# Holding the reads of turned blocks, row sums and meta probabilities until two to three gaps after an attention head

## The chip, the cores and the metric

The kernel runs on one core of one Trainium2 chip. Its engines work side by side, each through its own list of instructions in order: TensorE (PE, matmuls), VectorE (DVE), ScalarE (ACT), GpSimd (POOL) and SyncE (SP). SP only issues DMA transfers. An engine that waits for a semaphore holds everything behind it on its own list. The metric is the device time of one execution in microseconds; several runs are given by their median.

## The reference

Two layers of a decoder trunk over 512 tokens and 16 learned meta tokens put ahead of them, width 1024, float32. Per layer:

```
h = rmsnorm(x)
[u_pool | z_pool | c_q | c_kv | k_rope | z_mla | g_pool | g_mla] = h @ W_in
y_pool = W_pool_up( pool_mix(u_pool) * silu(z_pool) )
y_mla  = W_mla_up( mla(c_q, c_kv, k_rope) * silu(z_mla) )
x = x + W_out( sigmoid(g_pool) * y_pool + sigmoid(g_mla) * y_mla )
```

`mla` is causal attention with 8 heads: queries and keys of 64 + 32 features (32 of them rotary), values of 64, the query and key rows normalised, a softmax over all earlier tokens and the meta tokens. The result drops the meta positions.

## The kernel before

All activations lie transposed, features on the 128 partitions and the 528 tokens along the free axis. To keep float32 accuracy at a fast matmul rate, each operand is split into a rounded high part and the rest, and each product is three matmuls (`mm3`, lines 202 to 204): high by high, high by low, low by high. `wload` (line 189) does that for a 128x512 tile of weights: a DMA brings `raw` (line 133, three buffers), ScalarE makes `whi` (line 197), VectorE makes `wlo` (line 198).

The large products of both layers stand in one list, and `stream` walks it as a generator, a few matmuls at a step. The attention heads are written around it: wherever a head would have to wait, it calls `gap`, which advances the generator by a set amount of planned time (`FILL`, 2620 and 2530 ns in layers 0 and 1). `clk` adds up this planned time; `after(ns, fn)` puts a function on a list that `step` runs once `clk` has passed its time. So the program text is emitted as a mixture of heads and products. A scheduler then sets the order on each engine from its own estimate of when things are ready; the order is fixed in the program before it runs. `behind(a, b)` makes instruction `a` wait for instruction `b`; `newest[0]` is the last matmul that `mm3` emitted.

One head (`head`, line 805) goes like this. TensorE makes the scores of the four blocks of 128 queries against all their keys, VectorE masks them and finds the row maxima (`top`, line 824), ScalarE takes the exponential and sums the rows into `rs` (`expo`, line 831). `turn` (line 833) copies the 16 meta columns into `pm` on POOL (line 834) and transposes the rest on VectorE in squares of 32x32 into `attD` (line 837; one buffer). The squares reach their right partitions through DRAM: four stores `pdr<-attD` (line 899) and one read `attE<-pdr` of 640 KB (line 901; two buffers). The row sums go to DRAM as a row, `rdr<-rs` (line 894, 2 KB), and come back spread over 64 partitions, `cq<-rdr` (line 902, the tile `rb`). After an odd head `meta_turn` (line 909) sends the meta probabilities of the pair the same way: `mdr<-cq` (line 916) and three reads `racc<-mdr` (line 918). Then POOL multiplies the gate `z` by the reciprocal row sums (line 906), which waits for `cq<-rdr`.

Between heads, `prep` (line 783) moves parts of keys and queries with small transfers (`kh`, `kl`, `qhl`, lines 797 to 801). One head later `parts` (line 921) splits what was read into `attE`, and `pv` (line 932) multiplies it with the values; after an odd head, some time later, a matmul with `racc` (line 965) adds the meta part, and the result is multiplied by `z` (line 969).

All of these transfers, and the weight loads, stand on SP's one list. Each transfer signals one of eight semaphores in turn, so a transfer also waits for the one eight before it.

At the very start `WARM` matmuls of ones (line 155) run while the first data are on their way.

Of the kernel before, what the change touches and what calls it, by code (L numbers as in the profile page):

```python
# [9 lines left out]
F32 = mybir.dt.float32  # L10
F32R = mybir.dt.float32r
# [7 lines left out]
P = 128  # L19
# [3 lines left out]
NM = 16  # L23
T = SEQ + NM
# [30 lines left out]
LAG = 2000.0  # L55
TAIL = (9000.0, 9000.0)
SPL = 240
RET = 12500.0
WARM = 8
NB = 10  # L60


# [16 lines left out]
def trunk(ctx, tc, xT, xrow, mrow, pos, win, wkr, wqb, wkb, wvb, wgr, wpu, wmu, wout, gains, const, yT):  # L79
    nc = tc.nc  # L80
    pe, act, dve, gp, sp = nc.tensor, nc.scalar, nc.vector, nc.gpsimd, nc.sync
# [11 lines left out]
    def nm(s):  # L93
        uid[0] += 1
        return f"{s}_{uid[0]}"

    def slot(tag, dt=F32, bufs=1, w=W):
        return sl.tile([P, w], dt, tag=tag, name=nm(tag), bufs=bufs)
# [4 lines left out]
    def att(tag):  # L103
        return sl.tile([P, NB * P], F32 if tag == "D" else F32R, tag=f"att{tag}", name=nm(f"att{tag}"), bufs=1 if tag == "D" else 2)

    def wide():
        return tp.tile([P, NB * P], F32R, tag="th", name=nm("th"), bufs=2)
# [45 lines left out]
    wps = pp.tile([P, 512], F32, tag="o", name="wps", bufs=1)  # L153
    for i in range(WARM):
        pe.matmul(wps[:, 0:P], ones, ones, start=True, stop=True)
# [51 lines left out]
    newest = [None]  # L207
# [60 lines left out]
    def after(ns, fn):  # L268
        pend.append((clk[0] + ns, fn))
        pend.sort(key=lambda e: e[0])  # L270
# [32 lines left out]
    def behind(ins, other):  # L303
        tc.add_manual_dep(ins.ins, other.ins.name,
                          mybir.DependencyInfo(mybir.DependencyClass.Sync, mybir.DependencyReason.DATA))
# [35 lines left out]
    class Layer:  # L341
# [58 lines left out]
        def norm_sums(self):  # L400
# [51 lines left out]
            self.inv, self.cinv = slot("rinv"), slot("q1")  # L452
            fill_now(RET / 2)
            if self.l == 0:
                tables()
            fill_now(RET / 2 if self.l else RET / 4)
            for i, d in enumerate((self.inv, self.cinv)):
# [347 lines left out]
        def head(self, h, kq, prev):  # L805
            kh, kl, qh, ql = kq
            odd = h % 2
            nqs = self.nqs
            pa, pb, pc = slot("pa", w=416), slot("cq8"), slot("cq10")
            bia = sm.tile([P, 5], F32, tag="bia", name=nm("bia"), bufs=2)  # L810
            rs = sm.tile([P, 5], F32, tag="rs", name=nm("rs"), bufs=2)
            if odd == 0:
                self.pm = sm.tile([P, 4, 32], F32, tag="pm", name=nm("pm"), bufs=2)
                self.rb = slot("cq11")
            pm, rb = self.pm, self.rb
            blocks = att("D")
            grid = blocks.rearrange("p (b s r) -> p b s r", b=4, s=NB)

            def scores(i, out, a, b):
                q0 = NM + P * i  # L820
                return mm3(out, qh[:, q0:q0 + P], ql[:, q0:q0 + P], kh[:, a:b], kl[:, a:b], True, True)

            def top(i, c, sv, mask):
                return dve.tensor_tensor_reduce(out=sv, in0=sv, in1=mask, scale=nqs[:, i, h:h + 1], scalar=3e38,  # L824
                                                op0=ALU.add, op1=ALU.min, accum_out=bia[:, c:c + 1])

            def causal(n):
                return maskw[:, 512 - n:]

            def expo(i, c, sv, pv):  # L830
                act.activation(pv, sv, AF.Exp, scale=-1.0, bias=bia[:, i:i + 1], accum_out=rs[:, c:c + 1])  # L831

            def turn(i):
                gp.tensor_copy(pm[:, i, 16 * odd:16 * odd + 16], pt[i][:, 0:NM])  # L834
                for j, n in ((0, i + 1),) if i in (0, 1, 3) else ((0, 2), (2, 1)):
                    k = block(i, j)
                    ins = dve.transpose(grid[:, :, k:k + n, :].rearrange("p b s r -> p s b r"), pt[i][:, NM + P * j:NM + P * (j + n)])  # L837
                    if i in (1, 2):
                        behind(ins, newest[0])

            pt = [pa[:, 0:144], pa[:, 144:416], pb[:, 0:400], pc[:, 0:T]]
            sa = sct()
            s1, s3 = sa[:, 0:272], sa[:, 272:272 + SPL]
            scores(1, s1, 0, 272)
            scores(3, s3, 0, SPL)
            top(1, 1, s1, causal(272))
            top(3, 4, s3, maskw[:, 0:SPL])
            sb = sct()
            s2 = sb[:, 0:400]
            scores(2, s2, 0, 400)  # L850
            top(2, 2, s2, causal(400))
            expo(1, 1, s1, pt[1])
            expo(2, 2, s2, pt[2])
            if h == 1:
                self.spread_rope(1)
            if odd == 0 and h + 2 < H:
                self.spread_k(h // 2 + 1)
            self.gap()
            turn(1)
            turn(2)  # L860
            self.pv(prev)
            if h == 2:
                self.rope_keys(1)
            if odd and h + 1 < H:
                behind(self.keys(h // 2 + 1), newest[0])
            self.gap()
            sc = sct()
            s0, s4 = sc[:, 0:144], sc[:, 144:144 + T - SPL]
            scores(3, s4, SPL, T)

            def passes(out, q0, n):
                return [lambda k=k, q=q, x=x: pe.matmul(out, q[:, q0], x[:, 0:n], start=k == 0, stop=k == 2)
                        for k, (q, x) in enumerate(((qh, kh), (qh, kl), (ql, kh)))]

            todo = passes(s0, slice(NM, NM + P), 144)
            if not self.last:
                sm_ = sc[0:NM, 432:432 + NM]
                todo += passes(sm_, slice(0, NM), NM)
            for fn in todo:
                fn()  # L880
            if not self.last:
                dve.tensor_add(self.smeta[:, h, :], sm_, cst[0:NM, C_MM:C_MM + NM])
            top(3, 3, s4, causal(T - SPL))
            top(0, 0, s0, causal(144))
            dve.tensor_tensor(out=bia[:, 3:4], in0=bia[:, 3:4], in1=bia[:, 4:5], op=ALU.min)
            expo(3, 4, s3, pt[3][:, 0:SPL])
            expo(3, 3, s4, pt[3][:, SPL:T])
            expo(0, 0, s0, pt[0])
            turn(3)
            turn(0)  # L890
            dve.tensor_add(rs[:, 3:4], rs[:, 3:4], rs[:, 4:5])
            dve.reciprocal(rs[:, 0:4], rs[:, 0:4])
            row = rdr[self.l][h]
            sp.dma_start(row.rearrange("a (p i) -> p (a i)", i=4), rs[:, 0:4])
            got = att("E")
            n = NB * 32
            via = pdr[h % 2]
            for a in range(4):
                sp.dma_start(via[:, n * a:n * a + n].rearrange("(b k) x -> k b x", k=32),
                             blocks[32 * a:32 * a + 32, :].rearrange("p (b x) -> p b x", x=n))  # L900
            sp.dma_start(got.bitcast(F32), via)
            sp.dma_start(rb[64 * odd:64 * odd + 64, 0:512], row.partition_broadcast(64))
            if odd == 1:
                self.meta_turn(pm)
                z = self.zms[h // 2][:, NM:T].rearrange("p (i q) -> p i q", i=4)
                gp.tensor_mul(z, z, rb[:, 0:512].rearrange("p (q i) -> p i q", i=4))  # L906
            return h, got

        def meta_turn(self, pm):
            t = slot("cq9", F32R)  # L910
            f, hi, lo = t[:, 0:P], t[:, P:2 * P], t[:, 2 * P:3 * P]
            dve.transpose(f.bitcast(F32), pm.rearrange("p i r -> p (i r)"))
            split(hi, lo, f.bitcast(F32), 0, P)
            self.mt = slot("racc", F32R)
            via = mdr[0]
            sp.dma_start(via, t[:, P:3 * P].bitcast(F32))
            for g, c in ((0, 0), (32, 1), (64, 0)):
                sp.dma_start(self.mt[g:g + 32, 0:512].bitcast(F32).rearrange("p (a x) -> p a x", a=4),
                             via[:, P * c:P * c + P].rearrange("(a r) x -> r a x", a=4))

        def parts(self, prev):
            if prev is None:
                return None
            h, got = prev
            hi, f = wide(), got.bitcast(F32)
            for a in (0, NB * 64):
                b = a + NB * 64
                behind(act.activation(hi[:, a:b], f[:, a:b], AF.Copy), newest[0])  # L928
                dve.tensor_sub(got[:, a:b], f[:, a:b], hi[:, a:b].bitcast(F32))  # L929
            return h, hi, got  # L930
# [333 lines left out]
```

## Time and profile before

| what | value |
|---|---|
| median of 3 runs | 771.3 us (768.76 to 771.66) |
| the profiled execution | 770.3 us |
| its span, first to last instruction | 768.5 us |
| TensorE matmuls | 757.2 us, 99% of the span |
| VectorE | 537.7 us, 70% |
| ScalarE | 393.3 us, 51% |
| POOL | 141.1 us, 18% |
| mean granted TensorE clock | 0.995 |
| bytes moved by DMA | 113.03 MB |

The profile was taken in one execution. PE are TensorE's matmuls and PEld its weight loads; SPq is SP's queue, where a row is the issue of a transfer and not the transfer itself. L12 is line 12 of the kernel before. `out<-in` names tiles without their buffer numbers. In a listing by time a row gives start and length in us, and in brackets the idle time ahead of it with what ended it. The attention stages run from about 175 to 315 us (layer 0) and 560 to 695 us (layer 1).

### The profile page before, as it was taken

How to read it: one execution, taken by the hardware profiler on the slowest of the kernel's cores; microseconds unless marked ns; L12 is line 12 of the kernel's file. 1: busy time of each engine (PE TensorE's matmuls, PEld its weight loads, DVE VectorE, ACT ScalarE, POOL GpSimd, SP SyncE). 2: the span in 40 equal slices, each digit the busy share in tenths (PEclk: the TensorE clock that was granted, in tenths of full speed). 3: DMA queues.
4: the chain of work that ended last, by engine and by line, in shares of the span. 5: the costliest groups of instructions: out<-in, count | busy, mean ns of one | idle time of the engine just before them, and what ended most of it. 6: DMA issues, size and time to landing. Idle time of an engine off the chain costs nothing.

```text
span 768.5 us, 14306 instructions
## 1 busy us (share of the span) xinstructions
PE 757.2 (99%) x5028; PEld 689.0 (90%) x5028; DVE 537.7 (70%) x1211; ACT 393.3 (51%) x864; POOL 141.1 (18%) x187
## 2 busy tenths in 40 slices
PE   9999999999999899999999999999999999999998
PEld 9999999999989899999997898887788788788887
DVE  4588787358889887684366477774578799776832
ACT  5755655545556555543255445455445556554320
POOL 2026404000101010052130264030001110112400
PEclk9999999999999999999999999999999999999999
DMA  7532323336765667425542323234457677673363
GB/s 261 181 109 84 100 80 104 118 124 165 200 201 164 179 201 204 141 83 147 177 143 93 114 83 100 80 89 132 127 158 197 197 207 206 187 214 105 121 196 108
DMA packets 77204, 113.03 MB, mean 147 GB/s; under 512 B 15382, under 2 KB 36246, under 8 KB 77132
## 3 DMA queue, kind: packets, MB, share of 16 engines
q1 hardware_dynamic: 76988, 111.86, 48.4%
q8 instruction: 39, 0.64, 0.3%
q14 instruction: 33, 0.27, 0.1%
q10 hardware_dynamic: 144, 0.26, 0.1%
HBM read 89.76 MB, written 15.86 MB: 137 GB/s over the span
## 4 chain that ended last, share of the span: by engine, by line
PE 85%; DVE 6%; DMA 5%; SPq 1%; issue 1%; ACT 1%; DVEq 0%; ACTq 0%
PE mm L202 26%; PE mm L204 25%; PE mm L203 25%; DMA raw<-win 2%; PE S L202 2%; PE S L204 2%; PE S L203 2%; DVE wlo L198 1%; DVE S L824 1%; DMA kh<-kh 1%; DMA pdr<-attD 1%; PE S L528 1%; PE o L950 1%; PE o L953 1%; DMA mdr<-cq 1%
## 5 line engine op out<-in xcount | busy, mean ns | idle before, releaser
L202 PE MATMUL mm<-hh,whi 128*128 128x264 f32 (+2 forms) x1072 | 338.9, 318 | 5.9 <-ACT whi L197 4.0
L204 PE MATMUL mm<-hh,wlo 128*128 128x264 f32 (+2 forms) x1072 | 338.4, 318 | 0.2 <-DVE wlo L198 0.2
L203 PE MATMUL mm<-hl,whi 128*128 128x264 f32 (+2 forms) x1072 | 337.9, 316 | 0.0
L198 DVE TENSOR_TENSOR wlo<-raw,whi 128x512 fp32r<-128x512 f32 (+2 forms) x242 | 172.5, 715 | 108.5 <-ACT whi L197 103.3
L197 ACT ACTIVATE whi<-raw 128x512 fp32r<-128x512 f32 (+2 forms) x242 | 144.4, 600 | 181.2 <-PE mm L203 126.8
L202 PEld LDWEIGHTS mm<-hh,whi 128*128 128x128 f32 x1072 | 202.7, 189 | 20.2 <-ACT whi L197 4.9
L203 PEld LDWEIGHTS mm<-hl,whi 128*128 128x128 f32 x1072 | 202.8, 189 | 12.4
L204 PEld LDWEIGHTS mm<-hh,wlo 128*128 128x128 f32 x1072 | 202.2, 189 | 12.7 <-DVE wlo L198 0.6
L834 POOL COPY pm<-cq 128x16 f32<-128x16 f32 x32 | 13.3, 416 | 216.5 <-ACT cq L831 216.5
L824 DVE CUSTOM_DVE_ANT_0 S<-S,maskw,nqs 128x240 f32<-128x240 f32 (+4 forms) x80 | 38.3, 499 | 2.3 <-PE S L204 1.7
L642 POOL TENSOR_TENSOR racc<-racc,tmp 128x264 f32<-128x264 f32 (+1 forms) x15 | 14.3, 957 | 134.8 <-ACT tmp L641 134.8
L1025 POOL TENSOR_TENSOR tmp<-tmp,xb 128x264 f32<-128x264 f32 (+1 forms) x24 | 27.1, 1142 | 55.2 <-DVE tmp L1023 53.3
L831 ACT ACTIVATE cq<-S,bia 128x400 f32<-128x400 f32 (+2 forms) x48 | 24.4, 512 | 25.0 <-DVE bia L824 11.9
L202 PE MATMUL mm<-cq,whi 128*128 128x264 f32 (+1 forms) x108 | 34.8, 322 | 0.0
L203 PE MATMUL mm<-th,whi 128*128 128x264 f32 (+1 forms) x108 | 34.7, 321 | 0.0
L202 PE MATMUL mm<-u,whi 128*128 128x264 f32 (+1 forms) x108 | 34.6, 321 | 0.0
L204 PE MATMUL mm<-cq,wlo 128*128 128x264 f32 (+1 forms) x108 | 34.6, 322 | 0.0
L203 PE MATMUL mm<-cq,whi 128*128 128x264 f32 (+1 forms) x108 | 34.6, 321 | 0.0
L204 PE MATMUL mm<-u,wlo 128*128 128x264 f32 (+1 forms) x108 | 34.5, 319 | 0.0
L837 DVE STREAM_TRANSPOSE attD<-cq 128x256 f32<-128x256 f32 (+2 forms) x48 | 21.3, 467 | 12.7 <-DMA pdr<-attD 7.2
L906 POOL TENSOR_TENSOR u<-u,cq 128x512 f32<-128x512 f32 x8 | 12.4, 1552 | 76.4 <-DMA cq<-rdr 26.9
L929 DVE TENSOR_TENSOR attE<-attE,th 128x640 fp32r<-128x640 f32 x32 | 25.1, 809 | 0.5 <-ACT th L928 0.5
(297 smaller groups left out, 1304.7 us busy)
## 6 DMA issues: line engine op xcount, KB each, us to landing
raw<-win SPq DMA_DIRECT2D x143, 256.0 KB, 3.3
pdr<-attD SPq DMA_DIRECT2D x64, 160.0 KB, 3.1
attE<-pdr SPq DMA_DIRECT2D x16, 640.0 KB, 4.9
raw<-wout SPq DMA_DIRECT2D x32, 256.0 KB, 2.9
raw<-wpu SPq DMA_DIRECT2D x16, 256.0 KB, 2.7
raw<-wmu SPq DMA_DIRECT2D x16, 256.0 KB, 2.5
raw<-wqb SPq DMA_DIRECT2D x12, 256.0 KB, 2.6
xb<-xT SPq DMA_DIRECT2D x8, 264.0 KB, 5.6
```

Source lines behind the costliest of these rows:

```text
L197: act.activation(hi[:, :n], raw[:, :n], AF.Copy)
L198: dve.tensor_sub(lo[:, :n], raw[:, :n], hi[:, :n].bitcast(F32))
L202: first = pe.matmul(out, wh, xh, start=start, stop=False)
L203: pe.matmul(out, wh, xl, start=False, stop=False)
L204: newest[0] = pe.matmul(out, wl, xh, start=False, stop=stop)
L642: self.acc_last = gp.tensor_add(self.acc[:, a:b], self.acc[:, a:b], t[:, :b - a])
L824: return dve.tensor_tensor_reduce(out=sv, in0=sv, in1=mask, scale=nqs[:, i, h:h + 1], scalar=3e38, op0=ALU.add, op1=ALU.min, accum_out=bia ...
L831: act.activation(pv, sv, AF.Exp, scale=-1.0, bias=bia[:, i:i + 1], accum_out=rs[:, c:c + 1])
L834: gp.tensor_copy(pm[:, i, 16 * odd:16 * odd + 16], pt[i][:, 0:NM])
L837: ins = dve.transpose(grid[:, :, k:k + n, :].rearrange("p b s r -> p s b r"), pt[i][:, NM + P * j:NM + P * (j + n)])
L929: dve.tensor_sub(got[:, a:b], f[:, a:b], hi[:, a:b].bitcast(F32))
L1025: gp.tensor_add(t[:, :b - a], t[:, :b - a], self.am[m][:, a:b])
```

## The change

`WARM` goes from 8 to 9. The store of the row sums is emitted behind the four stores of the squares. The reads of what was stored leave `head` and `meta_turn` for functions that are put on the list with `after`: `attE<-pdr` and `cq<-rdr` (with the multiply on POOL and the allocation of their tiles) 5200 ns of planned time after the head, which is two gaps; `mdr<-cq` 2600 ns after, and `racc<-mdr` 7800 ns after. Each of these transfers is made to wait for the newest matmul at the time when it is emitted. `head` returns a list that the function fills, and `parts` takes its tile out of that list.

```diff
+BACK = 5200.0
-WARM = 8
+WARM = 9
...
                 self.pm = sm.tile([P, 4, 32], F32, tag="pm", name=nm("pm"), bufs=2)
-                self.rb = slot("cq11")
-            pm, rb = self.pm, self.rb
+            pm = self.pm
...
             row = rdr[self.l][h]
-            sp.dma_start(row.rearrange("a (p i) -> p (a i)", i=4), rs[:, 0:4])
-            got = att("E")
+            got = []
...
             for a in range(4):
                 sp.dma_start(via[:, n * a:n * a + n].rearrange("(b k) x -> k b x", k=32),
                              blocks[32 * a:32 * a + 32, :].rearrange("p (b x) -> p b x", x=n))
-            sp.dma_start(got.bitcast(F32), via)
-            sp.dma_start(rb[64 * odd:64 * odd + 64, 0:512], row.partition_broadcast(64))
+            sp.dma_start(row.rearrange("a (p i) -> p (a i)", i=4), rs[:, 0:4])
             if odd == 1:
                 self.meta_turn(pm)
-                z = self.zms[h // 2][:, NM:T].rearrange("p (i q) -> p i q", i=4)
-                gp.tensor_mul(z, z, rb[:, 0:512].rearrange("p (q i) -> p i q", i=4))
+
+            def back():
+                got.append(att("E"))
+                behind(sp.dma_start(got[0].bitcast(F32), via), newest[0])
+                if odd == 0:
+                    self.rb = slot("cq11")
+                rb = self.rb
+                behind(sp.dma_start(rb[64 * odd:64 * odd + 64, 0:512], row.partition_broadcast(64)), newest[0])
+                if odd == 1:
+                    z = self.zms[h // 2][:, NM:T].rearrange("p (i q) -> p i q", i=4)
+                    gp.tensor_mul(z, z, rb[:, 0:512].rearrange("p (q i) -> p i q", i=4))
+
+            after(BACK, back)
             return h, got
...
             split(hi, lo, f.bitcast(F32), 0, P)
-            self.mt = slot("racc", F32R)
             via = mdr[0]
-            sp.dma_start(via, t[:, P:3 * P].bitcast(F32))
-            for g, c in ((0, 0), (32, 1), (64, 0)):
-                sp.dma_start(self.mt[g:g + 32, 0:512].bitcast(F32).rearrange("p (a x) -> p a x", a=4),
-                             via[:, P * c:P * c + P].rearrange("(a r) x -> r a x", a=4))
+
+            def back():
+                self.mt = slot("racc", F32R)
+                for g, c in ((0, 0), (32, 1), (64, 0)):
+                    ins = sp.dma_start(self.mt[g:g + 32, 0:512].bitcast(F32).rearrange("p (a x) -> p a x", a=4),
+                                       via[:, P * c:P * c + P].rearrange("(a r) x -> r a x", a=4))
+                    behind(ins, newest[0])
+
+            after(BACK / 2, lambda: behind(sp.dma_start(via, t[:, P:3 * P].bitcast(F32)), newest[0]))
+            after(1.5 * BACK, back)
...
             h, got = prev
+            got = got[0]
```

The order on SP's queue, as built, of an odd head (head 1 of layer 1): before, `rdr`, four `pdr`, `cq`, `mdr`, `attE`, `qhl`, three `racc`, `qhl`, three weight loads; after, four `pdr`, `rdr`, `qhl`, `mdr`, `attE`, `cq`, `qhl`, three weight loads, three `racc`.

## The prediction

> **What bounds the kernel now.** I read the page first, then TensorE's instructions in order of time at the places where it sat idle, then windows around these, and last the issues of SP's DMA queue ahead of them. "Head 3 of layer 0" is the pass of `head` with h = 3.
>
> ```profile
> PE 757.2 (99%) x5028; PEld 689.0 (90%) x5028; DVE 537.7 (70%) x1211; ACT 393.3 (51%) x864; POOL 141.1 (18%) x187
> ```
>
> TensorE bounds it at 99%, so this edit can only win stops of TensorE. In the attention stages there are four; the idle time ahead of a matmul, and what ended it, stand in the brackets:
>
> ```profile
> 214.32 0.39 PE L202 MATMUL mm<-hh,whi 128*128 128x264 f32 x1 [0.96 <-ACT whi L197]
> 261.66 0.39 PE L202 MATMUL mm<-hh,whi 128*128 128x264 f32 x1 [1.83 <-DVE tmp L655]
> 600.57 0.50 PE L202 MATMUL mm<-hh,whi 128*128 128x512 f32 x1 [1.89 <-ACT whi L197]
> 661.33 0.50 PE L202 MATMUL mm<-hh,whi 128*128 128x512 f32 x1 [1.17 <-ACT whi L197]
> ```
>
> Stop 1 falls at the end of head 1 of layer 0, stop 2 at the start of head 4 there; stops 3 and 4 at the end of heads 1 and 5 of layer 1. Now the windows (from:to, length, busy us and instructions of PE, PEld, DVE, ACT and POOL, granted clock, DMA):
>
> ```profile
> 6.00:10.50 4.50, 4.50 (x22) 4.50 (x22) 3.27 (x6) 3.16 (x6) 0.00 (x0) 1.00 0.96 303
> 10.60:15.00 4.40, 4.40 (x38) 4.40 (x38) 3.75 (x7) 3.14 (x6) 0.00 (x0) 1.00 1.00 381
> 263.17:266.58 3.41, 3.41 (x17) 3.41 (x17) 3.35 (x11) 2.28 (x9) 0.39 (x2) 0.50 0.58 133
> 601.09:604.50 3.41, 3.41 (x12) 2.94 (x12) 3.41 (x11) 3.33 (x10) 0.99 (x2) 0.50 0.27 82
> ```
>
> Right behind stops 2 and 3 the granted clock is 0.50 for 3.41 us, so each lost 1.7 us more; stops of 0.96 and 1.17 drew no such window. The four cost 5.85 + 3.4 = 9.25 us. Stops 1, 3 and 4 wait for a weight tile (`whi` is made of `raw`). What held its load shows on SP's queue, which issues in order (start, length, transfer):
>
> ```profile
> SPq L902 <- DMA rdr<-rs: 17.3, 10, 2.8
> 201.60 1.21 SPq L894 DMA_DIRECT2D rdr<-rs  x1
> 202.86 1.97 SPq L899 DMA_DIRECT2D pdr<-attD  x4
> ...
> 205.71 0.58 SPq L916 DMA_DIRECT2D mdr<-cq  x1
> ...
> 208.45 1.46 SPq L918 DMA_DIRECT2D racc<-mdr  x3
> 209.96 1.38 SPq L133 DMA_DIRECT2D raw<-win  x3
> ```
>
> ```profile
> 588.04 0.52 SPq L894 DMA_DIRECT2D rdr<-rs  x1
> 588.61 2.01 SPq L899 DMA_DIRECT2D pdr<-attD  x4
> 590.72 0.68 SPq L902 DMA_DIRECT2D cq<-rdr  x1
> 591.49 0.57 SPq L916 DMA_DIRECT2D mdr<-cq  x1
> ...
> 596.30 1.83 SPq L133 DMA_DIRECT2D raw<-win  x3
> ```
>
> Weight loads stand behind reads of what was stored a moment ago: the one at 209.96, and the one at 596.30 too, come after three `racc` reads that wait for `mdr` to land. Stop 2 is indirect:
>
> ```profile
> 243.14 0.42 SPq L916 DMA_DIRECT2D mdr<-cq  x1
> ...
> 247.66 1.27 SPq L918 DMA_DIRECT2D racc<-mdr  x3
> 252.75 1.58 SPq L899 DMA_DIRECT2D pdr<-attD  x3
> 257.49 0.64 DVE L837 STREAM_TRANSPOSE attD<-cq 128x256 f32<-128x256 f32 x2 [2.56 <-PE S L872]
> pdr<-attD SPq DMA_DIRECT2D x64, 160.0 KB, 3.1
> ```
>
> `racc` waits 4.5 us for `mdr`, and everything behind it is late, the `pdr` stores too: the last of them ends its issue at 254.33. There is one attD buffer, so the next turn must wait until they have read it (254.3 + 3.1 = 257.4; the label names a matmul on which the turn does not depend). VectorE idles 2.56 us and then returns a PSUM tile 1.83 us late (L655).
>
> **The change part by part.** Every engine keeps its instructions, but for one warm-up matmul; SP has 605 transfers in both. As built, some 25 matmuls in nine places swap neighbours. That adds no work, so 0; the bounds are one 0.4 us matmul (the length in the row just below) at each place, 3.6 us of both signs.
>
> *The holds.* The `attE`, `mdr`, `racc` and `cq` transfers (16, 8, 24, 16) now wait for a matmul. For each I took the matmul that releases it and its end in this trace: it is earlier than the old issue every time, by 2 to 10 us. The closest is the `racc` read of layer 1's head 1, which went before the load at 596.30, at 594.20; its matmul is
>
> ```profile
> 591.75 0.40 PE L204 MATMUL mm<-hh,wlo 128*128 128x512 f32 x1
> ```
>
> and ends at 592.15. The wait for the data still ends last, so the holds cost 0. Behind a hold stand weight loads; if a hold came to end last, each us of it would be a us for them.
>
> *The queue's new order* is the real change. In each head the `rdr` store goes behind the four `pdr` stores, and the `cq` read of it to behind the `attE` read. Even heads get the first weight load ahead of both reads; no stop of TensorE lies there, so 0 (if these loads had been late it would be a gain). Odd heads:
>
> Stop 3. The `pdr` stores take `rdr`'s place, 588.04 to 589.55 (0.5 each); `rdr` 590.05, `qhl` 590.7, `mdr` 591.3, `attE` 3.1 behind the last `pdr`, 592.6. `cq` waits for `rdr` to land; L is that time. The `racc` reads now stand behind the loads, so the load goes at 590.05 + L + 1.3 (issues of `cq` and `qhl`, a gap). This trace has no `rdr` behind four stores. Issued ahead of all four, above, it landed within 588.04 to 590.72, 2.7 us. Issued between them it took up to 4.8:
>
> ```profile
> 605.21 0.38 SPq L894 DMA_DIRECT2D rdr<-rs  x1
> ...
> 610.02 0.49 SPq L902 DMA_DIRECT2D cq<-rdr  x1
> ```
>
> I take 3.3, next to the 3.1 of a `pdr` store, with 2.7 and 4.8 kept as ends. The load goes at 594.65, 1.65 earlier. I count 1.3 of it, since it now runs closer to the large `attE` read. The idle time falls to 0.6, and 1.17 drew no slow window: gain 1.3 + 1.7 = 3.0 (0.15 at L = 4.8, 3.6 if cured).
>
> Against the new order speaks the Trainium skill, "DMA: Bandwidth & Descriptors", section "Queues, rings and completion order": a transfer's semaphore increment lands only after every earlier write of the same DMA engine. By it `rdr` cannot land before the four stores ahead of it, L is 2.6 at least, and the sum stays as it is; both rows, 2.7 and 4.8, agree.
>
> Stop 1. `pdr` 201.6 to 203.1, `rdr` 203.6, `qhl` 204.2, `mdr` 204.8. `mdr` took 208.45 − 205.71 = 2.7, so `racc` goes at 207.5 and the load at 209.1: gain 0.85 (0 to 0.96).
>
> Stop 2. The four stores of head 3 leave 0.7 to 1 us earlier, having `rdr` behind them, and `attE` and `mdr` no longer stand behind the `cq` read. I put `mdr` at 241.0, so `racc` at 245.5, 2.1 earlier. Head 4's stores, whose last one began at 253.8, then end their issue 2.3 to 3 us earlier, about 251.5, and have landed by 254.9, when VectorE wants the buffer (257.49 − 2.56). Stop 2 goes: gain 1.83 + 1.7 = 3.5 (0 to 3.5).
>
> Stop 4, head 5 of layer 1, and head 3 there:
>
> ```profile
> 625.52 4.35 DMA raw<-win
> 649.59 2.00 SPq L899 DMA_DIRECT2D pdr<-attD  x4
> ...
> 655.85 1.46 SPq L133 DMA_DIRECT2D raw<-win  x3
> ```
>
> The first store of head 5 waits for the semaphore of an earlier weight load, so the stores win nothing. `rdr` goes behind them at 651.5, the load at 651.5 + L + 1.1 = 655.9: no gain at L = 3.3, and each us of L beyond it costs one. Head 3's load (625.52) lies on the chain that ended last and is placed alike: 0, and the same price beyond.
>
> *VectorE in layer 1.*
>
> ```profile
> 615.00:630.00 15.00, 15.00 (x76) 12.58 (x75) 14.54 (x34) 7.63 (x20) 3.14 (x5) 1.00 0.78 223
> ```
>
> Behind stop 3 it is busy 14.54 of 15 us, 97%. The 3.0 us won there were also its time to catch up, and later tiles would come back late. I give back 1.0 (0 to 3.0).
>
> *POOL.* The multiply by the row sums, eight per run, moves behind the next head's copies. TensorE waits for POOL nowhere: 0. If the multiply came late it would hold the next even head's `cq` read and the load behind, where there is no stop.
>
> *The ninth warm-up matmul.*
>
> ```profile
> 1.05 3.78 PE L155 MATMUL wps<-ones 128*128 128x128 f32 x16 [1.05 <-DVE na L754]
> 5.18 0.99 PE L202 MATMUL S<-hh,th 128*128 128x264 f32 x2 [0.35 <-ACT hh L364]
> ```
>
> Eight take 3.78 us, one 0.47: it closes the gap of 0.35 and costs 0.12 at most. Up to 10.5 matmuls start at 4.9 per us, behind it at 8.6, so TensorE ran at half speed until there, whatever the clock column says. If the closed gap brings full speed one step of 3.41 us earlier, it gains 1.7. The ends are −0.12 and 1.7; I take 0.8, the middle. The Trainium skill, "TensorE: Matmul & The Clock Gate", Part 1, says the window of activity is about 3.4 us and free-running, so that the ramp varies from run to run; the two slow windows of this trace have that length.
>
> Sum: 0.85 + 3.5 + 3.0 − 1.0 + 0.8 = 7.15 off the profiled execution's own 770.3, 763.2. It is 1.0 below the median of 771.3; I put the forecast at 763.5.
>
> **The rivals.**
>
> A, late row sums, slower. If `rdr` behind four stores lands after L = 5.5, the `cq` read holds the loads of the odd heads. Stop 3 comes 0.55 later instead of going. Stop 4 grows by 2.15 to 3.3 and draws a slow window (1.7); head 3 of layer 1 the same, 2.2 + 1.7; stop 1 grows by 1.3 to 2.3, with 1.7. Less the 3.5 of stop 2: 0.55 + 3.85 + 3.9 + 3.0 − 3.5 = +7.8, 778. Stop 3 breaks even at L = 4.95, the whole near 4.7. For it speaks the 4.8; against it that ten such waits make only 17.3 us, the longest 2.8.
>
> B, given back. VectorE at 97% eats what layer 1 wins; stops 1 and 2 alone give 770.3 − 4.35 = 766, and with stop 2 half cured 768. Against it: the loads of stop 3 come late for VectorE as well, which splits them.
>
> C, it does not do what it says: `mdr` landing late sets `racc` and all behind as before, 770 to 771. Against it, `mdr` itself goes earlier in stops 1 and 2, and in stop 3 the load passes `racc`.
>
> D, all four stops go and the ramp shortens: 770.3 − 9.25 − 1.7 = 759.3.
>
> **How the numbers follow.** The forecast has 0.48 (761 to 766), D 0.10, B 0.16, C 0.11, A 0.15 (771 to 780). The range 759.5 to 773 leaves out half of D and most of A. Half a per cent, 3.9 us, is what a measurement of this kernel can tell: faster is the forecast, D and half of B, 0.66; the same is the other half of B and C, 0.19; slower is A, 0.15.
>
> **What would show it.** Right: no window of clock 0.50 in either attention stage; stops 2 and 3 gone or under 1.2 us; the holds ending last nowhere on SP. Wrong: SP waiting for matmuls ahead of the `attE` and `racc` reads with loads behind; `cq` reads that wait longer than 17.3 us in all; new stops in layer 1 at heads 3 and 5.

## The result, and the profile after

The changed kernel takes 775.54 us (median of 20 runs, 772.41 to 780.75), the kernel before 770.36 (20 runs beside it, 766.66 to 776.31): a ratio of 1.0081 with a 95% interval of 1.0063 to 1.0099. It is slower by 0.8%, where 763.5 was forecast, and lies outside the range of 759.5 to 773. The profiled execution took 775.7 us; its span is 773.9, 5.4 more than the span before. The page of the changed kernel, busy time of each engine:

```profile
PE 755.3 (98%) x5030; PEld 684.0 (88%) x5030; DVE 536.0 (69%) x1211; ACT 393.7 (51%) x864; POOL 142.7 (18%) x187
```

TensorE is busy 1.9 us less than before in a span that is 5.4 longer, so it stands still 7.3 us more. Where it does, in order of time (idle time ahead of a matmul and what ended it in brackets); lines of this kernel are counted by its own code, in which `whi` is made in L198, the row sums are stored in L900, and `attE` is read in L906:

```profile
212.23 0.39 PE L203 MATMUL mm<-hh,whi 128*128 128x264 f32 x1 [0.35 <-ACT whi L198]
259.24 0.39 PE L203 MATMUL mm<-hh,whi 128*128 128x264 f32 x1 [0.35 <-DVE tmp L656]
585.08 0.36 PE L203 MATMUL S<-kh,qhl 96*128 96x272 f32 x1 [1.11 <-DMA kh<-cq]
597.87 0.50 PE L203 MATMUL mm<-hh,whi 128*128 128x512 f32 x1 [2.13 <-ACT whi L198]
617.54 0.36 PE L203 MATMUL S<-kh,qhl 96*128 96x272 f32 x1 [1.65 <-DMA kh<-cq]
631.76 0.50 PE L203 MATMUL mm<-hh,whi 128*128 128x512 f32 x1 [2.41 <-ACT whi L198]
652.85 0.36 PE L203 MATMUL S<-kh,qhl 96*128 96x272 f32 x1 [2.04 <-DMA kh<-kh]
666.14 0.50 PE L203 MATMUL mm<-hh,whi 128*128 128x512 f32 x1 [1.45 <-ACT whi L198]
```

The first two lines are stops 1 and 2 of the forecast: 0.35 us each, where they were 0.96 and 1.83. In this execution layer 0 did nearly what was forecast. The other six lie in layer 1, 10.79 us together, where before had 1.89 and 1.17. The three `mm` lines wait for weight tiles at the ends of heads 1, 3 and 5; the three `S` lines are new, they wait for the copied keys (`kh`) at the starts of heads 2, 4 and 6. No half-clock window is left in the span, whose mean granted clock is 1.000 (0.995 before):

```profile
core 0: 773.9 us, clock 1.000
```

SP's waits (us in total, times, longest): first that of the `attE` read in the kernel before, then those of the `attE` and `cq` reads in the changed kernel:

```profile
SPq L901 <- DMA pdr<-attD: 9.2, 12, 1.3
```

```profile
SPq L906 <- DMA pdr<-attD: 23.4, 21, 2.8
SPq L910 <- DMA rdr<-rs: 2.8, 3, 1.3
SPq L906 <- PE mm L205: 0.9, 3, 0.3
```

The `cq` reads hardly wait for the row sums any more (2.8 us; 17.3 before), and the holds end last three times, for 0.9 us in all. The wait for the squares (`pdr`) grew by what the wait for the row sums fell: 26.5 us for the two together before, 26.2 now. So over the run neither late row sums nor holds are where SP lost time. What got slower are other transfers of the same queue in layer 1's attention, 560 to 690 us (times issued, KB, median us from issue to landing), first before, then after:

```profile
raw<-win SPq DMA_DIRECT2D x35, 256.0 KB, 3.8
kl<-kl SPq DMA_DIRECT2D x3, 132.0 KB, 2.8
kh<-kh SPq DMA_DIRECT2D x3, 132.0 KB, 4.0
```

```profile
raw<-win SPq DMA_DIRECT2D x32, 256.0 KB, 4.4
kl<-kl SPq DMA_DIRECT2D x3, 132.0 KB, 5.8
kh<-kh SPq DMA_DIRECT2D x3, 132.0 KB, 6.2
```

### The profile page after: what moved, and what is told of

Read it like the earlier page. It is cut to its first block, busy times and chain, and to the rows that moved or that the text cites. A ratio compares the mean times of both kernels' runs of the same rounds, so it can differ in the third digit from the quotient of the medians.

```text
span 773.9 us, 14316 instructions
## 1 busy us (share of the span) xinstructions
PE 755.3 (98%) x5030; PEld 684.0 (88%) x5030; DVE 536.0 (69%) x1211; ACT 393.7 (51%) x864; POOL 142.7 (18%) x187
## 4 chain that ended last, share of the span: by engine, by line
PE 78%; DVE 9%; DMA 8%; SPq 2%; issue 2%; ACT 1%; DVEq 0%; ACTq 0%
PE mm L203 23%; PE mm L205 23%; PE mm L204 23%; DMA raw<-win 3%; DMA pdr<-attD 3%; DVE wlo L199 2%; DVE attD L837 2%; PE S L203 1%; DVE S L824 1%; PE S L204 1%; PE S L205 1%; SPq L898 1%; DMA rdr<-rs 1%; DMA kh<-kh 1%; DVE tmp L656 1%
## 5 line engine op out<-in xcount | busy, mean ns | idle before, releaser
L199 DVE TENSOR_TENSOR wlo<-raw,whi 128x512 fp32r<-128x512 f32 (+2 forms) x242 | 174.5, 724 | 126.6 <-ACT whi L198 121.4
L198 ACT ACTIVATE whi<-raw 128x512 fp32r<-128x512 f32 (+2 forms) x242 | 144.3, 600 | 197.2 <-PE mm L204 129.1
L203 PE MATMUL S<-kh,qhl 96*128 96x272 f32 (+5 forms) x64 | 19.5, 317 | 7.3 <-DMA kh<-cq 3.7
```

Source lines behind the costliest of these rows:

```text
L198: act.activation(hi[:, :n], raw[:, :n], AF.Copy)
L199: dve.tensor_sub(lo[:, :n], raw[:, :n], hi[:, :n].bitcast(F32))
L203: first = pe.matmul(out, wh, xh, start=start, stop=False)
```

## The experiments

Runs of one kernel spread over 2 to 11 us and a trace shows one of them, so verdicts go by the ratio to the kernel before on the same chip (95% interval in brackets), and a trace is read for what waits for what.

Two theories stood at first. Theory 1: the gain of layer 0 stands and layer 1 loses 9.6 us, because in its even heads a weight load now follows at once upon the `pdr` stores, these land later, and the single attD buffer hands that on. Theory 2: layer 1's attention is bound by a chain of its own and gives back what reaches it early.

**One layer alone.** The new form for one layer, the form of before for the other:

```diff
+            new = self.l == 0        # e1;  self.l == 1 in e2, with WARM = 8
...
-            after(BACK, back)
+            if new:
+                after(BACK, back)
```

> The change in layer 0 alone, with the ninth warm-up matmul; layer 1 as before. Theory 1 (the loss is made in layer 1 by the moved transfers there, the gain in layer 0 stands by itself): along TensorE's program the changed kernel was 4.2 us ahead when layer 1's attention began and lost 9.6 there, so 770.4 - 4.2 = 766. Theory 2 (layer 1's attention is bound by a chain of VectorE work and DMA, and gives back whatever reaches it early): 770 or a little above, with stops of TensorE in layer 1 of 11 us or more.

Measured: 772.27 against 772.98, 0.9989 (0.9960 to 1.0018).

> The change in layer 1 alone, with eight warm-up matmuls; layer 0 as before. Theory 1: the whole loss and no gain, 770.4 + 9.6 = 780, with the stops for keys (S waits for kh) and for weight tiles of the changed kernel. Theory 2: 771 to 773.

Measured: 776.66, 1.0049 (1.0014 to 1.0083). Neither theory fits both. Layer 1 makes a loss, but about half of it; layer 0 by itself wins nothing that can be told from no change. The gain of layer 0 that the one trace showed is not a steady one: three more traces with the same layer 0 (this run, and the runs with the odd heads alone and without holds below) still have 0.8 to 1.6 us at stop 1 and 1.3 to 1.4 at stop 2, though no half-clock window there.

**The warm-up matmul alone.**

```diff
-WARM = 8
+WARM = 9
```

> The kernel before with nine warm-up matmuls and nothing else. If the closed gap of 0.35 us brings full speed one clock window earlier: 1.8 to 2.2 us less, 768.3, with the granted clock full from about 6.3 us and not from 10.6. If the earlier ramp was luck of that execution: 770.4, within 0.5.

Measured: 772.53, 0.9981 (0.9949 to 1.0013). The stretch from 6.0 to 10.5 us, in which before ran 22 matmuls, first with eight warm-up matmuls (the run of layer 1 alone), then with nine:

```profile
6.00:10.50 4.50, 4.50 (x38) 4.46 (x38) 3.53 (x6) 3.58 (x7) 0.00 (x0) 1.00 1.00 347
6.00:10.50 4.50, 4.23 (x34) 4.01 (x33) 2.94 (x5) 2.80 (x5) 0.00 (x0) 1.00 0.95 328
```

In the four traces with eight the stretch held 22, 38, 25 and 37 matmuls, in the twelve with nine 34 to 39. Early full speed is to be had with eight too, and came every time with nine: worth some 1.9 us (16 matmuls at 8.6 per us) in the executions that would have been late. The time alone cannot show a gain of that size.

**The store put back ahead.** All deferred reads stay; only the row sums' store changes place.

```diff
+            sp.dma_start(row.rearrange("a (p i) -> p (a i)", i=4), rs[:, 0:4])
             for a in range(4):
                 sp.dma_start(via[:, n * a:n * a + n].rearrange("(b k) x -> k b x", k=32),
                              blocks[32 * a:32 * a + 32, :].rearrange("p (b x) -> p b x", x=n))
-            sp.dma_start(row.rearrange("a (p i) -> p (a i)", i=4), rs[:, 0:4])
```

> The changed kernel with the store of the row sums put back ahead of the four pdr stores; all deferred reads stay. My forecast's rival A (row sums that land late behind four stores hold the queue): the loss goes, 766 or less. Theory 1 in its present form (what is new is the weight load that follows at once upon the stores in even heads, and the key copies behind it that land late): the stops for keys in heads 2, 4 and 6 of layer 1 stay and the time is 774 to 777.

Measured: 772.48, 0.9986 (0.9955 to 1.0016). The loss is gone, and with it theory 1 as it stood: in this kernel too the weight load follows at once upon the stores in even heads. Rival A foretold the cure too, but it cannot be the whole mechanism, since the `cq` reads of the changed kernel wait for the row sums 2.8 us in all. What is left to try is theory 3: the small store (128 pieces of 16 bytes) right behind the four large ones is what costs, by what it does to the transfers around it.

**The store alone put behind, in the kernel before.**

```diff
-            sp.dma_start(row.rearrange("a (p i) -> p (a i)", i=4), rs[:, 0:4])
             for a in range(4):
                 sp.dma_start(via[:, n * a:n * a + n].rearrange("(b k) x -> k b x", k=32),
                              blocks[32 * a:32 * a + 32, :].rearrange("p (b x) -> p b x", x=n))
+            sp.dma_start(row.rearrange("a (p i) -> p (a i)", i=4), rs[:, 0:4])
             sp.dma_start(got.bitcast(F32), via)
```

> The kernel before with one edit: the store of the row sums goes behind the four pdr stores; no read is deferred, nothing is held, eight warm-up matmuls. Theory 3 (the small store right behind the pdr stores, with a weight load behind it, makes the stores count as landed later in the even heads of layer 1; the single attD buffer hands that on to VectorE): slower by nearly all that the changed kernel lost, +4 to +8, with the turn of the next head 0.3 to 0.8 us later behind the first store in even heads, and stops for keys. Rival (the deferral of the reads, or where it lets weight loads go, makes the loss): 0, within 2.

Measured: 780.01 against 771.83, 1.0088 (1.0058 to 1.0119). This one line makes the whole loss, with nothing deferred and nothing held. In the built kernel it moves more than the store: the planner also puts the `cq` read behind the `attE` read in every head, where before it stood ahead of it in all but one.

**New form in the odd heads of layer 1 alone** (layer 0 wholly new):

```diff
+            new = self.l == 0 or odd == 1
```

> The changed kernel, but the even heads of layer 1 as before (row sums stored first or among the pdr stores, read at once). Theory 3: the loss sits in the even heads, so it goes: 768 to 772 against 773 of before. Rival (the odd heads' loads, which now run beside the large attE read): 777 to 779, stops for weight tiles at the ends of heads 1, 3 and 5 as in the changed kernel.

Measured: 774.50, 1.0036 (1.0008 to 1.0064), between the two expectations.

**The store on ScalarE's queue.** The changed kernel with one word changed:

```diff
-            sp.dma_start(row.rearrange("a (p i) -> p (a i)", i=4), rs[:, 0:4])
+            act.dma_start(row.rearrange("a (p i) -> p (a i)", i=4), rs[:, 0:4])
```

> The changed kernel with the store of the row sums issued by ScalarE, so that SP's queue has the four pdr stores and then the weight load (even heads) with nothing between. Theory 3: no loss, as with the store put first: 770 to 773 against 773 of before. Rival (a weight load at once behind the pdr stores costs, whatever stands between): 777 to 780.

Measured: 765.89 (765.05 to 767.04), 0.9914 (0.9886 to 0.9941). This kernel beats both. Its TensorE at stops 1, 3 and 4 (stop 2 is gone), and the window behind stop 4:

```profile
213.27 0.39 PE L203 MATMUL mm<-hh,whi 128*128 128x264 f32 x1 [0.66 <-ACT whi L198]
595.22 0.50 PE L203 MATMUL mm<-hh,whi 128*128 128x512 f32 x1 [0.70 <-ACT whi L198]
656.70 0.50 PE L203 MATMUL mm<-hh,whi 128*128 128x512 f32 x1 [2.43 <-ACT whi L198]
```

```profile
657.66:661.07 3.41, 3.41 (x13) 3.04 (x12) 2.91 (x12) 2.69 (x9) 0.81 (x2) 0.51 0.37 113
```

Stop 3 has 0.70 left; the forecast had 0.6. No stop above 0.2 us waits for keys in layer 1 any more. Stop 4 is worse than before and draws a half-clock window. Here too the planner's order changed with the edit (the `cq` read goes ahead of the `attE` read again in eleven of the sixteen heads). Against the run with the store put back ahead the order is the same on every engine, but for one weight load in SP's list and the store itself; that pair differs by 0.7% (0.9986 to 0.9914, on two chips, so give or take 0.4%).

**The holds taken out**, with the store on SP as changed:

```diff
-                behind(sp.dma_start(got[0].bitcast(F32), via), newest[0])
+                sp.dma_start(got[0].bitcast(F32), via)
```

and likewise for the `cq`, `mdr` and `racc` transfers.

> The changed kernel without the waits on a matmul at the attE, cq, mdr and racc transfers; they are still emitted later. If the holds end last nowhere, as the changed kernel's trace reads: 777 to 780, as the changed kernel on this scale. If they cost: 773 or less.

Measured: 772.81, 1.0017 (0.9995 to 1.0040), better than the changed kernel by 0.6%. What it means shows only with its counterpart, the second run without holds below.

**The store on ScalarE in the kernel before**, to see what the deferral is worth when the store is out of the way:

```diff
-            sp.dma_start(row.rearrange("a (p i) -> p (a i)", i=4), rs[:, 0:4])
+            act.dma_start(row.rearrange("a (p i) -> p (a i)", i=4), rs[:, 0:4])
             got = att("E")
```

> The kernel before with the store of the row sums issued by ScalarE, nothing deferred or held, eight warm-up matmuls. If taking this store off SP's queue is by itself what made the changed kernel with that edit 0.9% faster than before: 765 to 768 against 772. If the deferral of the reads brings it and only needed the store out of the way: 770 to 773.

Measured: 771.24 against 772.76, 0.9979 (0.9956 to 1.0003). Moving the store wins nothing sure by itself; with the rest of the change it wins 0.9%. So that rest (the deferral, the holds and the ninth warm-up matmul, not taken apart here) does win, some 0.65%, once the store is away.

**An extra store, in the place that is suspected.** The row sums go by ScalarE, and SP stores a copy into a tensor that nobody reads:

```diff
+            sp.dma_start(spare[h % 2][0:128], rs[0:128, 0:4])     # [0:1] in e11
             if odd == 1:
                 self.meta_turn(pm)
```

> The changed kernel with the row sums stored by ScalarE, and on SP, right behind the four pdr stores, an extra store of the same 128 by 4 numbers into a tensor that nobody reads. Theory 3 (a small store behind the pdr stores delays the notice that these have landed, whatever it holds): back to the loss, 776 to 780 against 772. Rival (the loss came from the row sums themselves landing late, for the cq read): 766, as without the extra store.

Measured: 779.84, 1.0097 (1.0074 to 1.0119).

> As the run before, but the extra store has one row of 4 numbers, one packet in place of 128. If the packets of the small store cost: 766 to 768. If one more transfer in the queue, with its own notices, is enough: 776 to 780.

Measured: 772.07, 0.9999 (0.9986 to 1.0012). So the loss needs no row sums that come late: with these on ScalarE, a store that nobody reads makes it as well. Without it 0.9914, with one packet 0.9999, with 128 packets 1.0097: one more transfer costs 0.85%, and 127 more packets in it about as much again. The queues of the two runs differ in layer 1 by one swap (`attE` and `cq` in head 1), in layer 0 by several. Both expectations of the one-packet run were wrong, the truth lies in the middle. Why a transfer of one packet costs that much was not separated; it takes SP's issue time (0.29 us each, 0.59 with 128 packets, medians) and moves the planner's order.

**The holds taken out, with the store on ScalarE**, both edits shown above in one kernel:

```diff
+            act.dma_start(row.rearrange("a (p i) -> p (a i)", i=4), rs[:, 0:4])
...
+                sp.dma_start(got[0].bitcast(F32), via)
```

> The changed kernel with the row sums stored by ScalarE and without the waits on a matmul. If the holds cost 0, as I had forecast: 766. If they cost what the run without holds seemed to win back (0.6%, 4 to 5 us): 761 to 763. If the order that the holds force is worth something: 768 to 772.

Measured: 768.76, 0.9951 (0.9936 to 0.9966): here the holds are worth 0.4% (0.9951 against 0.9914, whose intervals overlap a little), with the store on SP they cost 0.6%. A wait that cost by itself would do so both times. Taking them out lets the planner place the reads elsewhere (on SP, `racc` comes ahead of the three weight loads again in head 1 of layer 1, in both kernels), so this is more likely the price of an order than of the waits; that was not tried place by place.

**Even heads or odd heads.**

```diff
+            (act if odd == 0 else sp).dma_start(row.rearrange("a (p i) -> p (a i)", i=4), rs[:, 0:4])   # e13; odd == 1 in e14
```

> The changed kernel with the row sums of the even heads stored by ScalarE; the odd heads' store stays on SP behind the four pdr stores. With all of these stores on ScalarE the ratio to before was 0.991, with all behind the pdr stores 1.008. If the loss is made in the even heads (weight load right behind, key copies after it): 0.991 to 0.995. If it is made in the odd heads: 1.004 to 1.008. If in both alike: 1.000.

Measured: 772.00 against 773.48, 1.0002 (0.9974 to 1.0031).

> The mirror image: the odd heads' row sums stored by ScalarE, the even heads' by SP behind the four pdr stores. Loss in the even heads: 1.004 to 1.008. In the odd heads: 0.991 to 0.995. In both alike: 1.000.

Measured: 769.28, 0.9933 (0.9905 to 0.9961). The store behind in the odd heads alone costs 0.9% over the kernel with none there, in the even heads alone 0.2% (not to be told from nothing), in both 1.7%. Most of the loss is made in the odd heads, which theory 3 had not said. The two together cost 0.6% more than their sum, just more than the intervals allow for. The changed kernel and the one with the even heads' store on ScalarE are a close pair: TensorE's order is the same, and SP's but for the store and five `cq` reads, none of them in heads 2, 4 and 6 of layer 1; they differ by 0.8%.

What the store does to the queue can be seen in the 2.5 us that begin 3.5 us behind the first `pdr` store of a head, when the stores run out and the next transfers should run. Windows at heads 1, 3 and 5 of layer 1 (the last two columns are the DMA engines' busy share and GB/s): before, changed, store on ScalarE, and the extra store of 128 packets.

```profile
592.11:594.61 2.50, 2.50 (x16) 2.15 (x15) 1.39 (x4) 1.16 (x3) 0.69 (x1) 1.00 0.63 160
623.62:626.12 2.50, 2.50 (x15) 2.09 (x14) 2.50 (x8) 0.71 (x2) 0.35 (x1) 1.00 0.76 134
653.09:655.59 2.50, 2.50 (x17) 2.17 (x15) 2.50 (x8) 0.77 (x2) 0.00 (x0) 1.00 0.62 148
```

```profile
589.27:591.77 2.50, 2.50 (x15) 2.17 (x14) 1.16 (x5) 1.68 (x5) 0.40 (x2) 1.00 0.45 113
622.60:625.10 2.50, 2.50 (x18) 2.28 (x17) 2.50 (x9) 1.31 (x3) 0.00 (x0) 1.00 0.29 61
658.03:660.53 2.50, 2.50 (x18) 2.28 (x17) 1.51 (x7) 1.15 (x4) 0.00 (x0) 1.00 0.47 89
```

```profile
587.26:589.76 2.50, 2.50 (x13) 2.06 (x13) 2.44 (x9) 1.99 (x6) 0.73 (x1) 1.00 0.62 159
617.78:620.28 2.50, 2.50 (x17) 2.18 (x16) 2.50 (x8) 0.69 (x2) 0.31 (x1) 1.00 0.79 153
646.74:649.24 2.50, 2.50 (x15) 2.05 (x15) 2.50 (x7) 0.63 (x1) 0.00 (x0) 1.00 0.61 149
```

```profile
593.65:596.15 2.50, 2.50 (x13) 2.06 (x13) 2.50 (x9) 1.70 (x6) 0.00 (x0) 1.00 0.34 86
627.15:629.65 2.50, 2.50 (x18) 2.28 (x17) 2.30 (x9) 1.51 (x5) 0.00 (x0) 1.00 0.51 57
659.09:661.59 2.50, 2.50 (x13) 2.00 (x12) 2.50 (x7) 0.64 (x1) 0.00 (x0) 1.00 0.22 42
```

The means are 147, 88, 154 and 62 GB/s. They are not the price of the store by themselves, since the queue's order changes with it. Wherever the row sums' store stands behind the four on SP, the planner puts the `cq` read of 128 KB behind the `attE` read; before, and with the store on ScalarE, it goes ahead of it in these three heads. 128 KB in 2.5 us are 52 of the 59 GB/s by which the changed kernel falls short. Head 3 of layer 1 on SP's queue, before and changed:

```profile
620.12 1.97 SPq L899 DMA_DIRECT2D pdr<-attD  x4
622.20 0.68 SPq L902 DMA_DIRECT2D cq<-rdr  x1
...
624.65 0.34 SPq L901 DMA_DIRECT2D attE<-pdr  x1
...
625.52 1.41 SPq L133 DMA_DIRECT2D raw<-win  x3
```

```profile
619.10 2.09 SPq L898 DMA_DIRECT2D pdr<-attD  x4
621.30 0.62 SPq L900 DMA_DIRECT2D rdr<-rs  x1
...
624.31 0.34 SPq L906 DMA_DIRECT2D attE<-pdr  x1
624.74 0.49 SPq L910 DMA_DIRECT2D cq<-rdr  x1
...
625.91 1.44 SPq L134 DMA_DIRECT2D raw<-win  x3
```

With the extra store the `cq` read stays ahead of `attE` and the windows are low all the same, so the order is not all of it. The weight loads behind the store show the price more directly. In heads 2 and 4 of layer 1 one load stands at once behind the stores; the table has its time from issue to landing. In heads 3 and 5 the loads stand behind the reads; the table has how long after the head's first `pdr` store the first of them leaves SP. All in us:

| kernel | small store behind the four on SP in | load of head 2 | of head 4 | load of head 3 leaves after | of head 5 |
| --- | --- | --- | --- | --- | --- |
| before | no head | | | 5.40 | 6.26 |
| store on ScalarE | no head | 3.5 | 3.4 | 5.44 | 6.17 |
| odd heads' store on ScalarE | even heads | 5.0 | 4.4 | 5.55 | 5.03 |
| even heads' store on ScalarE | odd heads | 3.8 | 3.5 | 6.44 | 7.36 |
| changed | all heads | 5.0 | 4.4 | 6.81 | 7.43 |
| extra store of 128 packets | all heads | | 2.7 | 6.64 | 5.57 |

The even heads' store makes the loads of heads 2 and 4 land 0.9 to 1.5 us later, the odd heads' store makes those of heads 3 and 5 leave 1.0 to 1.4 us later than before. In the odd heads part of that is the `cq` read, which now takes its 0.5 us of issue ahead of the loads. In head 5 the read also waited for the row sums, and that wait lies on the chain that ended last:

```profile
656.70 4.03 DMA rdr<-rs
661.96 3.42 DMA raw<-win
```

So rival A's mechanism has a share there, which was not measured apart. The extra store does not fit the table wholly: behind it the load of head 4 landed in 2.7 us, and that of head 5 left early but took 8.0 us to land (6.6 with the store on ScalarE). Why 2 KB in 128 packets hold up some transfers behind them is not shown by any view.

## Why the prediction was wrong, and where it was right

**The holds cost 0.** Right as far as waits go: 0.9 us in three waits at the `attE` reads, none of them at `racc`. That they also fix an order, worth 0.4% one way and 0.6% the other, was not in the forecast.

**The queue's new order** is the step that failed. It priced the store's new place by L, the time in which the row sums themselves land, and there it was near: 3.3 taken, 3.1 the median in the changed kernel's attention of layer 1 (4.0 in head 5). Of the two rows that it calls agreeing with at least 2.6, the one of 2.7 has no large store ahead of it and could not test that. But over the run the `cq` read hardly waits for it. The price was paid by the transfers behind the store, and the sum had no term for them: loads that land 0.9 to 1.5 us later in even heads and leave 1.0 to 1.4 us later in odd ones, from the table above. The `pdr` store, the `attE` read, the weight loads and the key copies were all taken at the landing times that they had before. That the store's place makes the loss is shown; by what the queue holds those transfers up stays open.

**Even heads: 0.** Wrong. The store of the even heads alone costs little (0.9933 against 0.9914), but beside that of the odd heads 0.8% (1.0081 against 1.0002). The sum asked only whether a stop lay there, not what late key copies would do. Three new stops, 1.11, 1.65 and 2.04 us, stand at the starts of heads 2, 4 and 6; the copy of head 4 on SP, the next `kh<-cq` waiting for its landing:

```profile
612.91 0.54 SPq L798 DMA_DIRECT2D kh<-kh  x1
...
617.23 0.51 SPq L800 DMA_DIRECT2D kh<-cq  x1
```

4.32 us; in the kernel before the same pair lay 2.73 apart:

```profile
614.91 0.54 SPq L797 DMA_DIRECT2D kh<-kh  x1
...
617.64 0.51 SPq L799 DMA_DIRECT2D kh<-cq  x1
```

**Stop 3, gain 3.0.** Its load was issued at 592.37, 6.6 us behind the head's first store (585.77), just as forecast (594.65 behind 588.04). But the load landed after 4.7 us (3.5 before), and the matmul that uses it came 5.50 us behind its issue (4.27 before): a stop of 2.13 in place of 0.6. It drew no slow window, so 1.7 less 0.2 of the 3.0 came, by luck and not for the reason given. With the store on ScalarE the step holds (0.70).

**Stop 4 and head 3, 0.** Wrong: 1.45 and 2.41 us. For head 3 the 0 did not follow from the sum's own terms: the store 1.9 us behind the first one as in head 5, L = 3.3 and 1.1 put its load 6.3 us behind the first store, where it had left at 5.40; it came at 6.81. In head 5 the row sums took 4.0 us in place of 3.3, and the load left at 7.43 where 6.3 was forecast. The forecast named new stops there as a sign of being wrong, beside `cq` reads that wait longer than 17.3 us in all; the stops came, the waits did not.

**Stops 1 and 2, gain 4.35.** In the profiled execution both fell to 0.35 and the slow window went. In the run with layer 0 alone, 0.9989, that gain cannot be seen, and its trace keeps 1.0 and 1.4 us of the two stops. The forecast's sign of being right, no half-clock window in either attention stage, came too, in a slower kernel: the clock of one trace does not rank these kernels. The slowest, with the store put behind in the kernel before, has a mean granted clock of 1.000 as well, and the one with the store put back ahead 0.991.

**VectorE in layer 1, −1.0.** Too small. VectorE's waits for weight tiles from 560 to 680 us, before and after:

```profile
DVE wlo L198 <- ACT whi L197: 9.8, 5, 4.0
```

```profile
DVE wlo L199 <- ACT whi L198: 20.1, 6, 6.1
```

VectorE waits 10.3 us longer for the late loads, in line ahead of its work on the next head's keys. It also waits longer for the squares to leave the one attD buffer, 4.6 us in five times (1.4 in one before).

**The warm-up matmul, 0.8.** In line with the counts above, not shown by the time.

**The rivals.** The sign and nearly the time (778) of rival A came. Its mechanism did so only in part. L was 3.1 and 4.0 in heads 3 and 5, where A loses from about 4.7 on; late row sums do end last in head 5, but the extra store makes the loss with the row sums on ScalarE. The page of the Trainium skill that the prediction names for this queue, "DMA: Bandwidth & Descriptors", says in its section "Issuing engines are not separate DMA queues" that starting transfers from several engines saves only the time of issuing them. Here the move of one 2 KB store to ScalarE is worth 1.7% (1.0081 to 0.9914), about 13 us, where sixteen issues of 0.39 us (their median on SP) are 6.2. But the planner's order changed with the move, and with nearly the same order it is 0.7%, 5.6 us, so no run here decides against that.

## What to carry to other kernels

A small store of many packets is not free because nobody waits for it: price what stands behind it in its queue, and try it on another engine's queue, out of the way of the reads and loads that follow the large stores. When a change reorders a queue, take apart the deferral and the reorder before judging either: here the rest of the change won 0.65% and one moved line lost 0.9% by itself and 1.7% against its best place. Where a step is costed at nothing because no stop lies there now, ask how far the next consumers are from being late.

## What the runs showed of the hardware that was not expected

A weight load issued right behind a store of 128 pieces of 16 bytes, itself behind four stores of 160 KB, landed in 4.4 and 5.0 us, and without that store between in 3.4 to 3.8. It is not a rule: behind another store of the same shape one landed in 2.7. One packet in place of 128 cost half as much in time. Stops of 2.13 and 2.41 us in the changed kernel drew no half-clock window, while 1.83 and 1.89 had drawn one in the kernel before, so the length of a stop alone does not decide that.
